# Scan loop of a hybrid RWKV encoder layer: fill matmuls between the first chunk's products, small products on four column groups, and later loads

## The chip, the cores and the metric

The kernel runs on one core of one Trainium2 chip. The metric is the time of one execution on the device, in microseconds. The time before is the median of three runs. In the profile PE is TensorE (PEld its weight loads), DVE is VectorE, ACT is ScalarE, POOL is GpSimd, and SP is SyncE, whose work here is the issuing of DMAs. Dies do not matter with one core.

## The reference, cut to what matters

Two request groups (1024 and 256 tokens of width 1024) pass one encoder layer with shared weights. A layer is a mixer (a gated short convolution and a bidirectional RWKV-7 recurrence, both fed from one input projection), a gated convolutional FFN, and a gated embedding. The change lies in the recurrence:

```
def step(S, inp):
    r_t, w_t, kk_t, b_t, k_t, v_t = inp
    sa = einsum('bhvk,bhk->bhv', S, kk_t)
    S = S * w_t - sa[..., None] * b_t + v_t[..., None] * k_t
    return S, einsum('bhvk,bhk->bhv', S, r_t)
...
for d, (z, z_shift, rev) in ((0, forward), (1, reverse)):
    outs.append(_wkv_scan(r, w, kk, kk * a, kd, v, rev))
y = outs[0] + outs[1]
```

There are 8 heads of size 64, two directions and 1280 tokens.

## The kernel before, in words

**Order.** The kernel is one long program. Nearly every instruction goes through a small wrapper class (`Pin`, its line is L204 in the profile) that keeps each engine's instructions in the order in which the Python code issues them. So every engine is a queue written by hand, and the order of calls in the code is the order of the work. SyncE issues nearly all DMAs, in order as well: a DMA that has to wait holds up the ones behind it.

**Scan.** The recurrence is computed in chunks of 64 tokens. A step n treats one group of 128 tokens (two chunks) in one direction: ten forward steps (n = 0 to 9), then ten backward ones (10 to 19). Within a chunk the recurrence needs the inverse of a triangular 64 by 64 matrix for each head. Its two diagonal 32 by 32 blocks are inverted on GpSimd (`b_inv`, 31 rounds of one product and one addition); the block beside them is put together with two small matrix products.

The functions of a step, and the tiles by which the profile shows them:

- `a_t(n)`: TensorE transposes of the keys K into two PSUM tiles (`g<-cst,K`), two copies to ZL on ScalarE.
- `a_gram(n, h)`, for each half h of the heads: Gram products of the keys with LS (`g<-LS,K`), six evictions on VectorE (AT, LS, ZL for each parity); after the second half the diagonal blocks go out to DRAM (dA). At h = 0 it also loads the start value W.
- `load_u(n)`: the blocks come back in another layout (U); `b_inv(n)` inverts them (W, tm).
- `b_out(n)`, `b_back(n)`: the inverses go to DRAM (dW) and come back (MT). `b_d(n)` transposes one quadrant of MT on VectorE (Dm).
- `b_x2(n)`: 16 products of 32 by 32 (`g<-Dm,AT`), called X^2 here, with the copy to X2 (in the profile X) on ScalarE. `b_m21(n)`: 16 more (`g<-MT,X`), M21, copied into MT.
- For each of the two chunks ci, in sequence because the second uses the state that the first leaves: `c_p1` (`p<-SV,LS`, copy R), `c_keep` (the old state, Sc), `c_sa` (`y<-SV,LS` and `p<-R,MT`, copied into SV), `c_z` (`p<-SV,ZL` and `y<-SV,ZL`; VectorE then forms the next state in Sc and SV, ScalarE copies Y).
- `load_k`, `load_l`, `load_v`: the loads of K (one buffer), LS (four buffers) and SV (two buffers) for later steps, on SyncE.

Inside step n the code works on three steps: the products of step n, the return of the inverse of step n+1 (`b_out`, `b_back`, `b_d`), and the Gram products and the inverse of step n+2. K and LS of step n+3 are loaded. PSUM has a ring of four tiles g for `a_t`, `a_gram`, `b_x2` and `b_m21`.

**Fill.** Between these pieces `gap(us, g)` runs matmuls of another stage, the rest of the input projection (`mm<-U,wh` and `mm<-U,wl`, in units of three matmuls, 0.65 us by the planner's table for 512 columns). The planner scales each gap by `share`, which is the work left, less a reserve TAIL, over the steps left and over 18.6, the sum of a step's gaps; a debt carries what a gap ran too much or too little. Fill brings its own weight splits and evictions on ScalarE and VectorE, its own loads on SyncE, and the queued side work that `run_side` issues. A gap with g set also issues a piece of the group norm of an earlier token group (steps 11 to 19), whose loads `gn_load` go through SyncE too.

**The lines that the change touches.** `a_gram` (L1100) and `a_t` (L1128): the place at which a ZL tile is made. `b_x2` (L1191) and `b_m21` (L1203). The prologue before the loop (L1340 to L1366): two `a_t`, `a_gram`, `load_u`, `b_inv`. The loop over n (L1374): `load_l(n + 3)` at its start, then `b_x2`, `c_p1(n, 0)`, `a_t(n + 2)`, `b_m21`, `c_keep`, `a_gram(n + 2, 0)`, `c_sa`, `a_gram(n + 2, 1)`, `c_z`, `load_u(n + 2)`, `b_inv(n + 2)`, a gap of 3.2, and the second chunk between gaps of 1.0, 1.5, 5.5 and 7.4. In the last two steps, which have no step n+2, gaps of 0.8, 1.0 and 1.0 stand in the places of `a_t` and the two `a_gram`.

Of the kernel before, what the change touches and what calls it, by code (L numbers as in the profile page):

```python
# [5 lines left out]
F32 = mybir.dt.float32  # L6
# [6 lines left out]
D = 1024  # L13
# [46 lines left out]
class B:  # L60
# [5 lines left out]
    def sb(self, pool, shape, dt=F32, tag=None, bufs=None):  # L66
        kw = {} if bufs is None else dict(bufs=bufs)
        return pool.tile(shape, dt, name=tag, tag=tag, **kw)
# [57 lines left out]
def build(tc, I, O, dbg=None, upto=99):  # L126
    b = B(tc, I, O)
    nc = tc.nc
    sb = b.sb
# [926 lines left out]
    ZL = {}  # L1056
# [10 lines left out]
    def load_k(n):  # L1067
        if n < N:
            d, g = steps[n]
            st[n] = dict(K=sb(wk, [128, 8, 128], F32, "K", 1))  # L1070
            (G if n == 0 else SP).dma_start(st[n]["K"].rearrange("p (h c) x -> p h (c x)", c=2), d_bk[d][:, g, :].rearrange("(h p) x -> p h x", p=128))

    def load_l(n):
        if n < N:
            d, g = steps[n]
            c, q = (d_cq[nm, d][:, g * 128:(g + 1) * 128].rearrange("(h p) x -> p h x", p=128) for nm in "cq")
            L = [LS[n % 4][:, i].rearrange("p (h c) t -> p h (c t)", c=2) for i in range(3)]
            e = G if n == 0 else SP
            for par in range(2):
                e.dma_start(L[par][halves[par]], c[halves[par]])  # L1080
            e.dma_start(L[2], q)
# [18 lines left out]
    def a_gram(n, h):  # L1100
        d, g = steps[n]
        S = st[n]
        if h == 0:
            S["AT"] = sb(wk, [128, 8, 64], F32, "AT", 3)
            S["dA"] = dr.tile([32, 32, 32], F32, name="dA", tag="dA", bufs=2)
            S["W"] = sb(wk, [128, 8, 32], F32, "W", 2)
            SP.dma_start(S["W"], I["consts"][:, C_WI:C_N].rearrange("p (c j) -> p c j", c=8))
        K, L, Zl, AT = S["K"], LS[n % 4], ZL[n % 3], S["AT"]
        bc = lambda c: cst[:, c:c + 64].unsqueeze(1).broadcast_to((128, 4, 64))
        MS, MQ = bc(C_MS[d]), bc(C_MQ[d])  # L1110
        pss = [sb(pg, [128, 4, 128], F32, "g") for par in range(2)]
        us = slice(4 * h, 4 * h + 4)
        for u in range(4):
            for par in range(2):
                rw = halves[par]
                PE.matmul(pss[par][:, u, :], K[rw, 4 * h + u, :], L[rw, par::2 - par, 4 * h + u, :], start=True, stop=True)
        cc, qc = slice(0, 64), slice(64, 128)
        for par in range(2):
            rw, ow, co, qo, ps = halves[par], halves[1 - par], par * 64, (1 - par) * 64, pss[par]
            V.tensor_tensor(AT[rw, us], ps[rw, :, cc], MS[rw], ALU.mult)  # L1120
            V.tensor_tensor(L[ow, par, us], ps[ow, :, cc], MS[ow], ALU.mult)
            V.tensor_tensor(Zl[:, par, us, qo:qo + 64], ps[:, :, qc], MQ, ALU.mult)
            if h == 1:
                for hh in range(2):
                    q = par * 2 + hh
                    SP.dma_start(S["dA"][q * 8:q * 8 + 8].rearrange("u s t -> s u t"), AT[q * 32:q * 32 + 32, :, hh * 32:hh * 32 + 32])

    def a_t(n):  # L1128
        if n < 3:
            ZL[n] = sb(wk, [128, 2, 8, 128], F32, f"ZL{n}")  # L1130
        K, Zl = st[n]["K"], ZL[n % 3]
        pss = [sb(pg, [128, 8, 64], F32, "g") for par in range(2)]
        for u in range(8):
            for par in range(2):
                PE.transpose(pss[par][:, u, :], K[halves[par], u, :], ident[halves[par], halves[par]])
        for par in range(2):
            A.copy(Zl[:, par, :, par * 64:par * 64 + 64], pss[par])

    def load_u(n):
        Ut = st[n]["U"] = sb(wk, [128, 32, 32], F32, "U", 2)  # L1140
        for r in range(4):
            SP.dma_start(Ut[r * 32:(r + 1) * 32], st[n]["dA"])


    def b_inv(n):
        d, g = steps[n]
        S = st[n]
        Ut = S["U"]
        W = S["W"]
        for i in (range(31) if d == 0 else range(31, 0, -1)):  # L1150
            cs = slice(0, i // 4 + 1) if d == 0 else slice(i // 4, 8)
            js = slice(i + 1, 32) if d == 0 else slice(0, i)
            nc_, nj = cs.stop - cs.start, js.stop - js.start
            tm = sb(wk, [128, 8, 32], F32, "tm", 1)
            G.tensor_tensor(tm[:, cs, js], W[:, cs, i:i + 1].broadcast_to((128, nc_, nj)),
                            Ut[:, i:i + 1, js].broadcast_to((128, nc_, nj)), ALU.mult)
            G.tensor_tensor(W[:, cs, js], W[:, cs, js], tm[:, cs, js], ALU.add)
# [33 lines left out]
    def b_x2(n):  # L1191
        d, g = steps[n]
        S = st[n]
        c1, c2, r1, r2 = quads(d)
        ps = sb(pg, [128, 4, 128], F32, "g")[:, 0:2, :].rearrange("p a (b j) -> p (a b) j", j=32)
        X2 = S["X2"] = sb(wk, [128, 8, 32], F32, "X2", 1)
        for u in range(8):
            for par in range(2):
                PE.matmul(ps[r2[par], u, :], S["AT"][r1[par], u, c2], S["D"][r1[par], u, :], start=True, stop=True)
        for par in range(2):  # L1200
            A.copy(X2[r2[par]], ps[r2[par]])

    def b_m21(n):  # L1203
        d, g = steps[n]
        S, Mt = st[n], MT[n % 2]
        c1, c2, r1, r2 = quads(d)
        ps = sb(pg, [128, 4, 128], F32, "g")[:, 0:2, :].rearrange("p a (b j) -> p (a b) j", j=32)
        for u in range(8):
            for par in range(2):
                PE.matmul(ps[r1[par], u, :], S["X2"][r2[par], u, :], Mt[r2[par], u, c2], start=True, stop=True)  # L1210
        for par in range(2):
            A.copy(Mt[r1[par], :, c2], ps[r1[par]])

    def chunks(n):
        return (0, 1) if steps[n][0] == 0 else (1, 0)
# [1 line left out]
    def c_p1(n, ci):  # L1217
        S, c = st[n], chunks(n)[ci]
        SV, L = S["SV"], LS[n % 4]
        ps1 = sb(pa, [128, 4, 64], F32, "p1")  # L1220
        for hp in range(4):
            for par in range(2):
                rw = halves[par]
                PE.matmul(ps1[rw, hp, :], L[:, par, 2 * hp + c, :], SV[:, c, par, hp, :], start=True, stop=True)
        R = S["R"] = sb(wk, [128, 4, 64], F32, "R", 1)
        A.copy(R, ps1)

    def c_keep(n, ci):
        S, c = st[n], chunks(n)[ci]
        Sc = S["Sc"] = sb(wk, [128, 4, 64], F32, "Sc", 1)  # L1230
        for par in range(2):
            A.copy(Sc[halves[par]], S["SV"][halves[par], c, par])
# [105 lines left out]
        SP.dma_start(d_ob[tk, :], v)  # L1338

    go(12.6)  # L1340
    a_t(0)
    for h in range(2):
        a_gram(0, h)
        go(1.2)
    load_u(0)
    b_inv(0)
    load_k(1)
    load_l(2)
    go(10.4)
    a_t(1)  # L1350
    for h in range(2):
        a_gram(1, h)
        go(1.2)
    load_u(1)
    load_k(2)
    b_inv(1)
    go(8.0)
# [9 lines left out]
    def gap(us, g=0):  # L1367
        k = max(1, round(us / 0.8))
        for _ in range(k):
            fill.run(us * share / k)  # L1370
            if g:
                next(gn, None)

    for n in range(N):  # L1374
        share = max(0.0, fill.left - TAIL) / (N - n) / 18.6
        nx, nx2 = n + 1 < N, n + 2 < N
        run_side()
        load_l(n + 3)
        if n == 4:
            gn_weights()  # L1380
        b_x2(n)
        c_p1(n, 0)
        if n >= 11:
            gn = group_norm(gl_g, gl_t)

        if nx2:
            a_t(n + 2)
        else:
            gap(0.8)
        b_m21(n)  # L1390
        c_keep(n, 0)
        if nx2:
            a_gram(n + 2, 0)
        else:
            gap(1.0)
        c_sa(n, 0)
        if nx2:
            a_gram(n + 2, 1)
        else:
            gap(1.0)  # L1400
        c_z(n, 0)
        if nx2:
            load_u(n + 2)
            b_inv(n + 2)
        if n >= 11:
            gn_load(gl_g, (2,))
        gap(3.2, 1)
        c_p1(n, 1)
        c_keep(n, 1)
        load_k(n + 3)  # L1410
        if nx:
            b_out(n + 1)
        gap(1.0, 1)
        c_sa(n, 1)
        if nx:
            b_back(n + 1)
        gap(1.5, 1)
        c_z(n, 1)
        fill.until(v_block + 1)
        if nx2:  # L1420
            load_v(n + 2)
        gap(5.5, 1)
        if nx:
            b_d(n + 1)
        gap(7.4, 1)
        for _ in gn:
            pass
        if n >= 10:
            gl_g = steps[n][1]
            gl_t = gn_load(gl_g, (0, 1, 3))  # L1430
# [644 lines left out]
```

## Time and profile before

| what | value |
|---|---|
| runs | 2170.63, 2177.81, 2175.63 us |
| median | 2175.63 us |
| profiled execution | 2179.25 us |
| its span, first to last instruction | 2177.5 us |
| mean granted TensorE clock | 0.993 |
| scan loop in the profiled execution | from 334 to about 884 us, 20 steps |

The rows of the profile read as follows. A timeline row has the start, the time from the first start to the last end, the engine, the operation, the tiles written and read, the shape and the count; in brackets the idle time before it and what ended it. A product with f32 operands of the small matrices appears as two passes, each with a weight load of its own, so 16 products are 32 rows. Matmuls overlap: the time that a group takes from the engine is the distance from its start to the next group's start. A row of the waits has the waiter, what it waited for, the total, the number of times and the longest. In a row of the stretches each engine's busy time is followed by its number of instructions, and the granted clock is a share of full speed.

### The profile page before, as it was taken

Reading aid. Unit: us, or ns where it says so; the run is one execution under the profiler, and the core shown is the slowest. Engines: PE = TensorE matmul, PEld = TensorE weight load, DVE = VectorE, ACT = ScalarE, POOL = GpSimd, SP = SyncE. Lnnn points to the kernel's source line nnn. Section 1 sums busy time; section 2 is a strip of 40 time slices with the busy share of each in tenths; the row PEclk is TensorE's granted clock in tenths of the full one; section 3 lists DMA queues with packets and bytes.
Section 4 is the critical chain, followed back from the end, with each engine's and each line's share of the span. In section 5 each row is a group of like instructions: output and inputs, shape, how many; then the busy total and the mean of one; then the engine's idle time right before and its main releaser. Section 6 shows DMA issues by size and latency. Waiting matters only on the chain.

```text
span 2177.5 us, 40081 instructions
## 1 busy us (share of the span) xinstructions
PE 2122.6 (97%) x15929; PEld 1842.6 (85%) x15929; DVE 1342.9 (62%) x2198; ACT 886.7 (41%) x1529; POOL 522.7 (24%) x1378
## 2 busy tenths in 40 slices
PE   6999999999999999999999999999999999999998
PEld 5877798888887787887889999999999888887886
DVE  5467823444445664565577677677777765556565
ACT  5556513333344444422455544444444511113444
POOL 4000046777776774000000000000000011125000
PEclk9999999999999999999999999999999999999999
DMA  4336675555566674635247422112223332233121
GB/s 154 111 102 179 178 209 126 129 139 133 124 180 179 177 195 139 234 124 168 96 131 205 141 77 76 64 64 77 70 76 121 145 109 87 87 114 114 44 85 54
DMA packets 345877, 273.16 MB, mean 125 GB/s; under 512 B 135549, under 2 KB 306907, under 8 KB 345691
## 3 DMA queue, kind: packets, MB, share of 16 engines
q1 hardware_dynamic: 332859, 245.96, 38.4%
q10 hardware_dynamic: 9632, 13.11, 1.7%
q0 software_dynamic: 3200, 11.54, 1.5%
q8 instruction: 125, 2.05, 0.4%
q14 instruction: 61, 0.50, 0.1%
HBM read 187.18 MB, written 83.36 MB: 124 GB/s over the span
## 4 chain that ended last, share of the span: by engine, by line
PE 60%; DVE 5%; DMA 3%; POOL 2%; issue 1%; ACT 1%; SPq 1%; ACTq 0%; DVEq 0%; POOLq 0%
PE mm L204 24%; PE X L204 13%; PE Y L204 10%; PE g L204 6%; PE m L204 3%; PE p L204 2%; POOL W L204 1%; POOL tm L204 1%; SPq L204 1%; DVE wl L204 1%; DVE h L204 1%; PE y L204 1%; PE tp L204 0%; DMA dW<-W 0%; DVE aj L204 0%
## 5 line engine op out<-in xcount | busy, mean ns | idle before, releaser
L204 PE MATMUL mm<-U,wh 128*128 128x512 f32 (+1 forms) x1872 | 519.4, 365 | 2.8 <-ACT U L204 2.3
L204 PEld LDWEIGHTS mm<-U,wh 128*128 128x128 f32 x1872 | 324.1, 189 | 68.7 <-issue 11.8
L204 PE MATMUL mm<-U,wl 128*128 128x512 f32 (+1 forms) x936 | 336.0, 359 | 1.0 <-POOL wl L204 1.0
L204 POOL TENSOR_TENSOR tm<-W,U 128x60 f32<-128x60 f32 (+24 forms) x620 | 200.4, 323 | 111.4 <-DMA U<-dA 63.6
L204 POOL TENSOR_TENSOR W<-W,tm 128x60 f32<-128x60 f32 (+24 forms) x620 | 214.4, 346 | 48.6
L204 PEld LDWEIGHTS mm<-U,wl 128*128 128x128 f32 x936 | 176.8, 189 | 29.4 <-POOL wl L204 1.6
L204 DVE TENSOR_TENSOR f<-f,mm 128x512 f32<-128x512 f32 x200 | 136.4, 686 | 101.5 <-PE mm L204 100.4
L204 POOL TENSOR_TENSOR MG<-raw,MG 128x1024 fp32r<-128x1024 f32 x5 | 12.1, 2413 | 654.2 <-ACT MG L204 654.2
L204 PE MATMUL X<-B,wh 128*128 128x384 f32 (+1 forms) x936 | 158.5, 315 | 2.9 <-DVE MGb L204 2.9
L204 DVE SCALAR_TENSOR_TENSOR h<-MGb,fcol,h 128x255 f32<-128x255 f32 (+1 forms) x176 | 152.6, 880 | 14.1 <-ACT h L204 12.3
L204 ACT CAST wh<-raw 128x512 fp32r<-128x512 f32 (+1 forms) x141 | 113.8, 808 | 116.4 <-PE Y L204 41.6
L204 PE MATMUL mm<-MG,act 128*128 128x512 f32 x600 | 158.6, 391 | 0.7 <-DVE f L204 0.6
L204 PEld LDWEIGHTS X<-B,wh 128*128 128x128 f32 x936 | 144.3, 189 | 3.4 <-DVE MGb L204 3.4
L204 PE MATMUL X<-B,wl 128*128 128x384 f32 (+1 forms) x804 | 137.2, 315 | 3.1 <-DVE MGb L204 2.9
L204 PEld LDWEIGHTS mm<-MG,act 128*128 128x128 f32 x600 | 112.9, 189 | 24.8 <-DVE f L204 1.4
L204 PEld LDWEIGHTS X<-B,wl 128*128 128x128 f32 x804 | 123.7, 190 | 3.7 <-DVE MGb L204 3.1
L204 PE MATMUL mm<-wh,MG 128*128 128x512 f32 x400 | 126.3, 394 | 0.0
L204 PE MATMUL g<-WG,MG 128*128 128x512 f32 x480 | 112.8, 391 | 0.0
L204 PEld LDWEIGHTS g<-WG,MG 128*128 128x128 f32 x480 | 89.4, 188 | 18.3
L204 DVE TENSOR_TENSOR AT<-g,cst 64x256 f32<-64x256 f32 x80 | 33.6, 420 | 106.9 <-PE g L204 105.9
L204 DVE TENSOR_TENSOR wl<-raw,wh 128x1024 fp32r<-128x1024 f32 (+1 forms) x68 | 75.2, 1106 | 34.8 <-ACT wh L204 34.4
L204 PEld LDWEIGHTS mm<-wh,MG 128*128 128x128 f32 x400 | 74.8, 187 | 18.5
(503 smaller groups left out, 4178.7 us busy)
## 6 DMA issues: line engine op xcount, KB each, us to landing
raw<-in_w_up SPq DMA_DIRECT2D x53, 512.0 KB
raw<-in_w_in SPq DMA_DIRECT2D x39, 512.0 KB
d_act<-h SPq DMA_DIRECT2D x22, 640.0 KB
MGb<-d_act SPq DMA_DIRECT2D x20, 640.0 KB
raw<-in_w_down SPq DMA_DIRECT2D x22, 512.0 KB
d_bk<-o SPq DMA_DIRECT2D x32, 320.0 KB
U<-dA SPq DMA_DIRECT2D x80, 128.0 KB
K<-d_bk SPq DMA_DIRECT2D x19, 512.0 KB
```

Of the source, the lines that this page charges most:

```text
L204: return lambda *a, **k: tc.keep_in_program_order(f(*a, **k))
```

## The change

1. X^2 and M21. So far the sixteen products write two column groups (32 partitions of PSUM each) and 256 columns. Now heads-and-chunks u = 0 to 3 go to the column groups used so far and u = 4 to 7 to the other two, in the order u, u + 4, so that products of both row groups and all four column groups follow one another; the result has 128 columns. The copy is split: ScalarE takes the first four, VectorE the other four.
2. Order of a step. `a_t(n + 2)` goes from between `c_p1(n, 0)` and `b_m21(n)` to behind `c_keep(n, 1)`. Gaps of 1.3, 0.6 and 1.0 come in before `b_m21`, before `c_sa(n, 0)` and before `c_z(n, 0)`; the gap behind `b_inv` shrinks from 3.2 to 2.4, those of 5.5 and 7.4 to 4.9 and 5.9. The sum stays 18.6. The special gaps of the last two steps are gone.
3. `load_l(n + 3)`, the three loads of LS, goes from the start of the step to behind `b_inv(n + 2)`.
4. Prologue: the first two `a_t` go behind the `a_gram` and `load_u` of their step (the first also behind `b_inv`).

```
     def b_x2(n):
-        ps = sb(pg, [128, 4, 128], F32, "g")[:, 0:2, :].rearrange("p a (b j) -> p (a b) j", j=32)
+        ps = sb(pg, [128, 4, 128], F32, "g")[:, 0, :].rearrange("p (b j) -> p b j", j=32)
-        for u in range(8):
-            for par in range(2):
-                PE.matmul(ps[r2[par], u, :], S["AT"][r1[par], u, c2], S["D"][r1[par], u, :], start=True, stop=True)
+        for u in range(4):
+            for v, r in ((u, r2), (u + 4, r1)):
+                for par in range(2):
+                    PE.matmul(ps[r[par], u, :], S["AT"][r1[par], v, c2], S["D"][r1[par], v, :], start=True, stop=True)
         for par in range(2):
-            A.copy(X2[r2[par]], ps[r2[par]])
+            A.copy(X2[r2[par], 0:4], ps[r2[par]])
+            V.tensor_copy(X2[r2[par], 4:8], ps[r1[par]])
...
     for n in range(N):
         run_side()
-        load_l(n + 3)
...
         b_x2(n)
         c_p1(n, 0)
+        gap(1.3)
...
-        if nx2:
-            a_t(n + 2)
-        else:
-            gap(0.8)
         b_m21(n)
         c_keep(n, 0)
         if nx2:
             a_gram(n + 2, 0)
-        else:
-            gap(1.0)
+        gap(0.6)
         c_sa(n, 0)
         if nx2:
             a_gram(n + 2, 1)
-        else:
-            gap(1.0)
+        gap(1.0)
         c_z(n, 0)
         if nx2:
             load_u(n + 2)
             b_inv(n + 2)
+        load_l(n + 3)
...
-        gap(3.2, 1)
+        gap(2.4, 1)
         c_p1(n, 1)
         c_keep(n, 1)
+        if nx2:
+            a_t(n + 2)
         load_k(n + 3)
...
-        gap(5.5, 1)
+        gap(4.9, 1)
         if nx:
             b_d(n + 1)
-        gap(7.4, 1)
+        gap(5.9, 1)
```

`b_m21` is changed as `b_x2` is, with the roles of r1 and r2 exchanged and the copies going into MT.

More of the change, by code (lines that the diff above doesn't have):

```diff
@@ L1103, in a_gram @@
         if h == 0:
+            if n < 3:
+                ZL[n] = sb(wk, [128, 2, 8, 128], F32, f"ZL{n}")
             S["AT"] = sb(wk, [128, 8, 64], F32, "AT", 3)
@@ L1128, in a_t @@
     def a_t(n):
-        if n < 3:
-            ZL[n] = sb(wk, [128, 2, 8, 128], F32, f"ZL{n}")
         K, Zl = st[n]["K"], ZL[n % 3]
@@ L1206, in b_m21 @@
         c1, c2, r1, r2 = quads(d)
[L1207 to L1210, printed above, removed]
+        ps = sb(pg, [128, 4, 128], F32, "g")[:, 0, :].rearrange("p (b j) -> p b j", j=32)
+        for u in range(4):
+            for v, r in ((u, r1), (u + 4, r2)):
+                for par in range(2):
+                    PE.matmul(ps[r[par], u, :], S["X2"][r2[par], v, :], Mt[r2[par], v, c2], start=True, stop=True)
         for par in range(2):
-            A.copy(Mt[r1[par], :, c2], ps[r1[par]])
+            A.copy(Mt[r1[par], 0:4, c2], ps[r1[par]])
+            V.tensor_copy(Mt[r1[par], 4:8, c2], ps[r2[par]])
     def chunks(n):
@@ L1340, in build @@
     go(12.6)
-    a_t(0)
     for h in range(2):
@@ L1346, in build @@
     b_inv(0)
+    a_t(0)
     load_k(1)
@@ L1349, in build @@
     go(10.4)
-    a_t(1)
     for h in range(2):
@@ L1354, in build @@
     load_u(1)
+    a_t(1)
     load_k(2)
```

## Prediction

> **What bounds the kernel now.** I read the page first, then the busy time by stretches with one stretch for each scan step, then TensorE's own timeline through step 9, and last the waits that end inside the loop. All edits are in the scan loop, so the page only has to say which engine to watch.
>
> ```profile
> span 2177.5 us, 40081 instructions
> ...
> PE 2122.6 (97%) x15929; PEld 1842.6 (85%) x15929; DVE 1342.9 (62%) x2198; ACT 886.7 (41%) x1529; POOL 522.7 (24%) x1378
> ```
>
> The columns of the stretches: limits, length, busy time of each engine, granted clock, DMA share, GB/s. Step 9 starts at 577.89, steps 12, 13 and 14 at the next three starts; the last row lies inside step 13.
>
> ```profile
> core 0: us, PE busy (x) PEld busy (x) DVE busy (x) ACT busy (x) POOL busy (x), PEclk, DMA share, GB/s
> 577.89:604.50 26.61, 26.48 (x350) 22.11 (x350) 15.01 (x28) 8.03 (x19) 21.75 (x63) 1.00 0.37 88
> 658.47:687.59 29.12, 26.98 (x357) 22.20 (x356) 15.79 (x35) 13.04 (x27) 20.03 (x62) 1.00 0.64 174
> 687.59:718.26 30.67, 29.63 (x359) 25.25 (x359) 19.51 (x41) 13.52 (x27) 22.32 (x62) 0.89 0.67 178
> 718.26:748.90 30.64, 28.70 (x366) 23.93 (x366) 18.81 (x40) 13.40 (x27) 21.36 (x60) 0.94 0.65 177
> ...
> 689.00:695.50 6.50, 6.50 (x130) 5.91 (x133) 3.06 (x5) 3.71 (x9) 5.48 (x14) 0.50 0.73 213
> ```
>
> In step 9 TensorE is busy 26.48 of 26.61 us, so an ordinary step is TensorE's instruction list from end to end: a gain must shorten that list. GpSimd, which does the 32-row inverses, is busy 21.75 us of the step and runs close behind. Steps 12 to 14 are 2.5, 4.1 and 4.0 us longer than step 9, and one stretch runs at clock 0.50: there are the real stalls, 10.6 us in all.
>
> TensorE's list in step 9 (start, time to the last end, form, count):
>
> ```profile
> 575.69 0.63 PE L204 MATMUL mm<-U,wh 128*128 128x512 f32 x2
> ...
> 576.39 0.63 PE L204 MATMUL mm<-U,wh 128*128 128x512 f32 x2
> ...
> 577.89 0.69 PE L204 MATMUL g<-Dm,AT 32*32 32x32 f32 x32
> 578.51 0.69 PE L204 MATMUL p<-SV,LS 128*64 128x64 f32 x16
> 579.13 0.71 PE L204 MATMUL g<-cst,K 64*128 64x64 f32 x16
> 579.77 0.69 PE L204 MATMUL g<-MT,X 32*32 32x32 f32 x32
> 580.39 1.27 PE L204 MATMUL g<-LS,K 64*128 64x128 f32 x16
> 581.60 0.27 PE L204 MATMUL y<-SV,LS 64*64 64x64 f32 x2
> ...
> 582.24 1.16 PE L204 MATMUL g<-LS,K 64*128 64x128 f32 x16
> 583.33 0.69 PE L204 MATMUL p<-SV,ZL 128*64 128x64 f32 x16
> ...
> 584.41 0.50 PE L204 MATMUL mm<-U,wh 128*128 128x256 f32 x2
> ...
> 587.58 1.04 PE L204 MATMUL p<-SV,LS 128*64 128x64 f32 x16
> 588.55 0.73 PE L204 MATMUL mm<-U,wh 128*128 128x512 f32 x2
> ...
> 590.13 0.27 PE L204 MATMUL y<-SV,LS 64*64 64x64 f32 x2
> ...
> 590.75 0.73 PE L204 MATMUL mm<-U,wh 128*128 128x512 f32 x2
> ```
>
> In order: X^2 (b_x2), c_p1, the transposes of a_t, M21, the Gram products of half 0, c_sa, Gram half 1, c_z, fill; then the second chunk's c_p1 and c_sa between fill. Start to start these take 0.62, 0.62, 0.64, 0.62, 1.21, 0.64, 1.09, 1.08 us. Each counted matmul is one pass; 32 passes are 16 instructions of the program.
>
> **The change, part by part.** Negative is a gain.
>
> (A) *X^2 and M21 on four column groups.* Same passes, four array tiles in flight instead of two. Turn time from the rows: c_z runs its 32 passes of 64 columns on two tiles, 16 turns, in 1.08 us; c_p1 has 8 such turns in 0.62. The difference gives 0.0575 us a turn and 0.16 us fixed. X^2 has 16 turns of 32 columns in 0.62, so 0.029 us a turn. Does a turn hold four tiles for the price of two? The second chunk's c_sa answers: it runs 32 passes of 64 columns on a 2 by 2 set of tiles, from 590.13 to 590.75, 0.62 us, exactly c_p1's 0.62 for half as many passes. So four tiles fit, each row group feeding two column groups, as the new loops have it. X^2 then takes 8 x 0.029 + 0.16 = 0.39, a gain of 0.23; twice a step, 20 steps: **-9.2**. The other end is 0, if passes cannot start faster than X^2's present one per 0.016 us. The row of c_sa is one per 0.014 at twice the columns, so I take the whole gain. The Trainium skill, "TensorE: Matmul & The Clock Gate", section "Wait — 56ns, not 53.3ns?", has a floor of about 25 ns between matmul starts; by it nothing would be gained here and the sum below would be +0.7 instead of -8.5; but 32 passes in 0.62 us are under that floor already, so the trace does not agree.
>
> (B) *Fill between the first chunk's products.* a_t is taken out from between c_p1 and M21, and fill goes in at three places (before M21, before c_sa, before c_z). The total is unchanged, 18.6 in units of a step, so only the added entries cost. An entry is priced in step 18, where fill already stands between c_p1 and M21:
>
> ```profile
> 831.70 0.72 PE L204 MATMUL mm<-U,wh 128*128 128x512 f32 x2
> ...
> 832.59 0.69 PE L204 MATMUL g<-MT,X 32*32 32x32 f32 x32
> ```
>
> Three matmuls take 0.89 there and 0.70 in the stream (575.69 to 576.39): 0.19 an entry, 3 x 0.19 x 18 steps = **+10.3**. Steps 18 and 19 already had the three. If the 0.6 gap is often empty it is +6.8. a_t costs TensorE the same 0.64 in its new place.
>
> (C) *The second chunk's c_p1.* At 587.58 it takes 0.97 to its successor, not 0.62. What it waits for:
>
> ```profile
> 587.94 0.54 PEld L204 LDWEIGHTS p<-SV,LS 128*64 128x64 f32 x14 [0.20 <-DVE SV L204]
> ...
> 581.59 0.42 DVE L204 TENSOR_TENSOR AT<-g,cst 64x256 f32<-64x256 f32 x1 [3.61 <-PE g L204]
> ...
> 586.48 0.41 DVE L204 TENSOR_TENSOR Sc<-p,Sc 128x256 f32<-128x256 f32 x1
> 586.92 0.97 DVE L204 TENSOR_TENSOR SV<-Sc,pend 64x256 f32<-64x256 f32 x2
> ```
>
> VectorE starts the first Gram eviction at 581.59 and works without a break through twelve of them, Sc and SV until 587.89: 6.3 us after Gram half 0, while TensorE needs 587.58 - 581.60 = 6.0 to arrive. In the new order TensorE needs, from the same point, 0.79 (0.6 of fill and an entry) + 0.64 + 1.09 + 1.19 + 1.08 + 2.59 = 7.4. The wait of 0.35 is covered by 1.1 us, unless fill's own VectorE work, now issued between the evictions, eats it. 0.35 in some 15 steps is 5.3; bounds 0 and -5.3; I take 70%, **-3.7**.
>
> (D) *First-half waits.* Gram half 0 takes 1.21, half 1 1.09 for the same sixteen passes: its second PSUM tile is one that a_t filled just before and ScalarE still empties. With a_t in the second chunk the four-deep ring comes round to tiles long free: 0.12 x 18 = **-2.2**. In the backward steps c_sa takes 0.79 (below) against 0.64, as it waits for M21's copies; fill now stands before it and VectorE takes half of them: 0.15 x 8 = **-1.2**.
>
> ```profile
> 608.21 0.27 PE L204 MATMUL y<-SV,LS 64*64 64x64 f32 x2
> ...
> 609.00 1.16 PE L204 MATMUL g<-LS,K 64*128 64x128 f32 x16
> ```
>
> (E) *The queue of SyncE.* Three loads of LS move behind the twelve of W, dA and U (SyncE, all DMAs in order) and ahead of K and dW. a_t issues no DMA, but load_k now waits for its transposes, 0.64 us after c_p1; behind that wait stand K and dW, and for dW wait MT, Dm, and X^2 of the next step.
>
> ```profile
> 594.44 2.56 SPq L204 DMA_DIRECT2D dW<-W  x4
> 598.80 1.80 SPq L204 DMA_DIRECT2D MT<-dW  x4
> ...
> 664.58 1.28 SPq L204 DMA_DIRECT2D LS<-d_c  x2
> 665.90 0.60 SPq L204 DMA_DIRECT2D LS<-d_q  x1
> ...
> 676.34 2.55 SPq L204 DMA_DIRECT2D dW<-W  x4
> ...
> 684.93 1.82 SPq L204 DMA_DIRECT2D MT<-dW  x4
> ```
>
> ```profile
> PE g L204 <- DVE Dm L204: 4.5, 5, 2.1
> ...
> ACT R L204 <- DMA LS<-d_c: 3.8, 1, 3.8
> ```
>
> LS costs the queue 1.9 us. In step 12 it stands before dA when the queue is already late, so dA and U come up to 1.9 us earlier now; but dW keeps its place behind LS, so the end of the chain moves little. In step 12 dW took 684.93 - 678.89 = 6.0 us to land against 1.8 in step 9, X^2 came late and the clock fell to 0.50. In step 14 ScalarE's R stood 3.8 us behind a landing of LS that now comes at another time. These are collisions in the DMA queues: some will go, others come. Their sum is the 10.6 us of the three steps and a part of the 2.4 us by which the waits for Dm exceed their longest (4.5 less 2.1); I count 1.4 of these, so 12.0. Bounds: -12 and, by the slower rival, +16. I take a third back, **-4.0**.
>
> (F) *New copies on VectorE.* Four a step, each at most the 0.42 of an eviction twice as wide; before Gram half 0 VectorE is idle (3.61 us ahead of 581.59), and 1.3 us of fill and c_p1 lie between X^2 and M21. Where group norm is queued ahead (steps 11 to 19) M21 can wait: between 0 and 0.97 (two queued operations such as SV's) x 8 = 7.8; I take **+1.5**, as 0.62 + 1.49 us of work cover most.
>
> (G) *Prologue.* The two first a_t move behind their Grams; no fill is added, bound one a_t either way, 0.64. I take 0.
>
> Sum: -9.2 + 10.3 - 3.7 - 2.2 - 1.2 - 4.0 + 1.5 = -8.5. The profiled execution took 2179.25 us (span 2177.5), so 2170.75 there; it lies 3.6 above the median of the three runs, 2175.63, and against that median the forecast is **2167.1 us**.
>
> **The rivals.**
>
> *Packing gains nothing.* X^2's passes already start 0.016 us apart (half of a turn's 0.029 us), and if starts are limited by issue there, four tiles change nothing. Against it stands c_sa's 0.014 with columns twice as long. Sum -8.5 + 9.2 = +0.7: 2176.3. The floor named in (A) is of this kind.
>
> *The late stalls all go.* For it: the queue is 1.9 us freer before dA just where it is late. Then (E) is -12.0 and (C) -5.3, sum -18.1: 2157.5.
>
> *Slower: LS in front of dW.* In every step dW is now issued directly behind LS and K, 1.9 us later in the queue, and may land as slowly as in step 12, 4.2 us later. This row is the slack at step 10, which starts at 604.50:
>
> ```profile
> 602.06 0.44 DVE L204 STREAM_TRANSPOSE Dm<-MT 32x256 f32<-32x256 f32 x1 [0.65 <-DMA MT<-dW]
> ```
>
> 2.0 us. It decides once 1.9 plus the added landing time exceeds 2.0; at the full 6.1, X^2 is 4.1 late. Half of that in eight backward steps is +16, and (E)'s -4 falls away: sum -8.5 + 4 + 16 = +11.5: 2187.1. Against it: GpSimd is busy 21.75 of a step's 26.61 us, so the end of an inverse, rather than the queue, mostly lets dW go.
>
> That the change does not do what it says is excluded: all its instructions are issued in a fixed order.
>
> **How the numbers follow.** A measurement of this kernel tells about 0.3%, 6.5 us, from no change. Chances: my sum, give or take 5 us, 0.60 (two thirds of it more than 6.5 below); packing gains nothing 0.12; late stalls all go 0.16; slower 0.12. Faster by over 0.3%: 0.40 + 0.16 = 0.56; slower 0.12; the rest, 0.32, is within. The range runs from the second rival, 2157, to just past the first with a small share of the third, 2179; left out are most of the slower rival and what lies below all-stalls-gone, under 2 in 10.
>
> **What would show it.** X^2 and M21 at 0.39 start to start instead of 0.62 (A); fill between M21 and c_sa with three matmuls in 0.89 (B); the second chunk's c_p1 at 0.62 (C); Gram half 0 at 1.09 (D); ordinary steps about 0.3 us shorter than now; in the waits, TensorE behind Dm at or under 4.5 us. Wrong would be X^2 still at 0.62, or Dm waits in many steps with SyncE's dW later than 16 us after the step's start.

## The result and the profile after

The changed kernel is slower: 2200.51 us (median of five, 2196.18 to 2203.96) against 2172.76 us (median of five) before, a ratio of 1.0127 with a 95% interval of 1.0112 to 1.0141. That is 27.7 us more, where 8.5 less was forecast. The profiled execution took 2200.83 us; the one before lies 6.5 above its median, so the two profiles are only 21.6 us apart. The span after, then the stretches of five steps (9, 7, 11, 12, 13, each from one X^2 to the next) and 2 us out of step 7; the columns are those of the table of stretches in the prediction:

```profile
span 2199.0 us, 40124 instructions
```

```profile
580.57:607.66 27.09, 26.45 (x350) 21.55 (x349) 16.05 (x32) 7.63 (x19) 22.16 (x63) 1.00 0.44 113
524.30:554.08 29.78, 27.96 (x341) 22.21 (x340) 14.25 (x28) 8.31 (x20) 22.17 (x66) 0.94 0.47 126
634.96:666.79 31.83, 27.06 (x357) 21.35 (x357) 15.81 (x38) 13.23 (x27) 20.72 (x64) 0.99 0.58 163
666.79:697.69 30.90, 29.38 (x356) 23.15 (x356) 18.93 (x42) 12.51 (x26) 19.90 (x60) 0.90 0.60 167
697.69:731.06 33.37, 31.01 (x360) 24.82 (x360) 20.79 (x45) 13.11 (x27) 20.39 (x58) 0.85 0.59 160
529.60:531.60 2.00, 2.00 (x19) 1.78 (x17) 0.58 (x2) 1.31 (x4) 1.61 (x6) 0.50 0.96 294
```

Step 9, an ordinary step, takes 27.09 us (26.61 before), where 0.3 less was expected. Steps 11 to 13 take 31.83, 30.90 and 33.37 (26.90, 29.12 and 30.67 before). Seven steps, 11 to 17, carry most of the loss: from X^2 of step 11 to X^2 of step 18 it is 854.22 - 634.96 = 219.3 us, against 829.68 - 631.57 = 198.1 before, 21.2 us more. Among the steps before these, step 7 alone loses 3.2. The same seven steps as one stretch, after and then before:

```profile
634.96:854.22 219.26, 201.45 (x2488) 159.72 (x2489) 132.14 (x294) 91.09 (x187) 147.60 (x426) 0.93 0.60 167
631.57:829.68 198.11, 192.63 (x2490) 159.90 (x2489) 121.51 (x263) 94.45 (x187) 146.41 (x420) 0.97 0.68 184
```

Of the 21.2 us, 12.3 are standing (17.8 against 5.5). The other 8.8 are busy time: TensorE takes that much longer for the same number of matmuls, at a mean granted clock of 0.93 instead of 0.97. So a part of the cost is slower matmuls, as in step 7 below, behind a stand.

What TensorE waited for, in all:

```profile
PE g L204 <- DVE Dm L204: 14.5, 12, 3.5
...
PE g L204 <- ACT X L204: 5.6, 6, 1.8
```

Dm was late for 4.5 us in the whole run before, and now for 14.5. The copies of X are a wait that the page before did not have.

**Where the copies hurt.** Step 7, all engines but SyncE, in order of time:

```profile
523.15 3.21 DVE L204 SCALAR_TENSOR_TENSOR cvy<-cvp,pcol,cvy 128x1282 f32<-128x1282 f32 x2
...
524.30 0.45 PE L204 MATMUL g<-Dm,AT 32*32 32x32 f32 x32
...
524.83 0.26 ACT L204 COPY X<-g 32x128 f32<-32x128 f32 x1 [5.79 <-PE g L204]
...
526.28 1.34 DVE L204 TENSOR_TENSOR wl<-raw,wh 128x1024 fp32r<-128x1024 f32 x1
...
527.55 0.68 DVE L204 TENSOR_TENSOR cvy<-mm,cvy 128x512 f32<-128x512 f32 x1
...
528.26 0.28 DVE L204 COPY X<-g 32x128 f32<-32x128 f32 x1
...
528.57 0.26 ACT L204 COPY X<-g 32x128 f32<-32x128 f32 x1 [3.48 <-DVE X L204]
...
528.86 0.29 DVE L204 COPY X<-g 32x128 f32<-32x128 f32 x1 [0.32 <-ACT X L204]
...
528.88 0.76 PE L204 MATMUL g<-MT,X 32*32 32x32 f32 x30 [1.75 <-ACT X L204]
...
529.57 2.08 PE L204 MATMUL g<-LS,K 64*128 64x128 f32 x16
```

X^2 is through at 524.7. ScalarE copies its first quarter at once. VectorE has a convolution, a weight split and an eviction of fill queued ahead, and takes its first quarter at 528.26, 3.5 us later. ScalarE's second quarter then stands 3.48 us behind VectorE's first: the four copies go one after another, ScalarE, VectorE, ScalarE, VectorE. TensorE stands still for 1.75 us, the clock falls to 0.50 (last row of the stretches), and the Gram half behind it takes 2.08 instead of 1.16.

**Where the loads hurt.** Step 11. GpSimd's inverse, then SyncE's issues, then what SyncE waited for between 652 and 661, then TensorE's first product of step 12:

```profile
647.08 0.29 POOL L204 TENSOR_TENSOR W<-W,tm 128x8 f32<-128x8 f32 x1
653.56 0.36 POOL L204 TENSOR_TENSOR tm<-W,U 128x31 f32<-128x31 f32 x1 [6.20 <-DMA U<-dA]
```

```profile
649.33 1.71 SPq L204 DMA_DIRECT2D U<-dA  x4
651.08 1.24 SPq L204 DMA_DIRECT2D LS<-d_c  x2
652.36 0.61 SPq L204 DMA_DIRECT2D LS<-d_q  x1
653.01 0.51 SPq L204 DMA_DIRECT2D cvy<-d_v  x1
653.62 0.41 SPq L204 DMA_DIRECT2D K<-d_bk  x1
659.87 2.56 SPq L204 DMA_DIRECT2D dW<-W  x4
663.92 1.87 SPq L204 DMA_DIRECT2D MT<-dW  x4
```

```profile
SPq L204 <- DMA d_thr<-gth: 5.8, 1, 5.8
```

```profile
666.79 0.31 PE L204 MATMUL g<-Dm,AT 32*32 32x32 f32 x2 [3.50 <-DVE Dm L204]
```

The inverse that dW waits for ends at 647.37, but dW goes out at 659.87, 12.5 us later. U, LS, cvy and K stand ahead of it, and between K and dW SyncE waits 5.8 us until another transfer has landed (the profile names an output of fill, issued by ScalarE; in the trace that output and the first transfer of dW report to the same semaphore, so the wait is probably for its reuse, which no run tests). In step 11 before, it went out 3.1 us behind the inverse's end at 642.86, straight behind K:

```profile
645.35 0.53 SPq L204 DMA_DIRECT2D K<-d_bk  x1
645.97 2.71 SPq L204 DMA_DIRECT2D dW<-W  x4
```

Over the nine inverses of steps 11 to 19, dW went out 1.30 us behind the end of the inverse on average before, and 6.40 now; over the nine of steps 2 to 10 it was 0.31 and 2.09. The landing did not get slower: from the last issue of dW to the first of MT it took 2.6 us on average before and 2.2 after, in steps 11 to 19.

### The profile page after: what moved, and what is told of

It reads as the page before. It is cut to its first block, busy times and chain, and to the rows that moved or that the text cites. A ratio compares the mean times of both kernels' runs of the same rounds, so it can differ in the third digit from the quotient of the medians.

```text
span 2199.0 us, 40124 instructions
## 1 busy us (share of the span) xinstructions
PE 2128.9 (97%) x15929; PEld 1832.7 (83%) x15929; DVE 1366.9 (62%) x2278; ACT 878.7 (40%) x1529; POOL 521.6 (24%) x1378
## 4 chain that ended last, share of the span: by engine, by line
PE 62%; DVE 6%; DMA 4%; POOL 2%; ACT 2%; issue 2%; SPq 1%; ACTq 0%; POOLq 0%; DVEq 0%
PE mm L204 25%; PE X L204 13%; PE Y L204 10%; PE g L204 7%; PE m L204 3%; PE p L204 2%; SPq L204 1%; POOL W L204 1%; POOL tm L204 1%; PE y L204 1%; DMA dW<-W 1%; DMA MT<-dW 1%; DVE wl L204 1%; DMA U<-dA 1%; DMA dA<-AT 1%
## 5 line engine op out<-in xcount | busy, mean ns | idle before, releaser
L204 PE MATMUL mm<-U,wh 128*128 128x512 f32 (+1 forms) x1872 | 529.3, 370 | 2.8 <-ACT U L204 2.3
L204 PEld LDWEIGHTS mm<-U,wh 128*128 128x128 f32 x1872 | 323.1, 190 | 71.3 <-issue 12.5
L204 PE MATMUL Y<-B,wh 128*128 128x384 f32 x420 | 85.1, 335 | 0.0
```

Source lines behind the costliest of these rows:

```text
L204: return lambda *a, **k: tc.keep_in_program_order(f(*a, **k))
```

## The experiments

Ratios are to the kernel before, with their 95% intervals. The first theory has two causes: the divided copies, and the loads of LS ahead of dW. The rival is the rest of the change: packing, the moved transposes, and fill cut into more pieces. "After" is the changed kernel, "before" the old one.

**Undoing each in the changed kernel.** Three versions of after: all eight copies on ScalarE (a_act), the loads of LS back at the start of the step (a_ls), and both (a_act_ls); and before with the packing alone (b_pack_act, all copies on ScalarE).

```
a_act        -            V.tensor_copy(X2[r2[par], 4:8], ps[r1[par]])
             +            A.copy(X2[r2[par], 4:8], ps[r1[par]])       (and the same for MT)
a_ls         -        load_l(n + 3)      (behind b_inv(n + 2))
             +        load_l(n + 3)      (behind run_side())
```

> The changed kernel with all eight copies of X^2 and M21 back on ScalarE. Theory 'copies' (the halves on VectorE wait behind its queue, and because the four copies read one PSUM bank they run ScalarE, VectorE, ScalarE, VectorE in turn; M21 is late and everything behind it): most of the 27.7 us over the kernel before goes, about 2178 to 2186, and M21's waits for X go. Theory 'loads' (LS in front of K and dW makes Dm late): 5 us at most go, about 2196, and the waits of TensorE for Dm stay near 15 us.

> The changed kernel with the three loads of LS back at the start of the step. Theory 'loads': about 2175 to 2183, TensorE's wait for Dm falls from 14.5 us to under 6. Theory 'copies': under 6 us go, about 2195, waits for Dm and X stay. A third theory, 'fill' (fill between the first chunk's products brings weight loads and VectorE work ahead of dA), expects little from this run and from the one with the copies on ScalarE.

> Both: copies on ScalarE and LS at the start of the step. If 'copies' and 'loads' are the whole cause, the forecast's structural sum shows: 2163 to 2172, under the kernel before. Theory 'fill': stays above 2180.

> The kernel before with X^2 and M21 on four column groups and nothing else, all copies on ScalarE. X^2 at 0.38 us start to start. If packing is worth its full price, 2162 to 2166 (0.24 us twice a step, 9.6 us). If the longer copies (four of 0.26 us for two of 0.37) delay M21, which has only c_p1 and a_t before it, 2168 to 2174.

Measured: a_act 1.0067 (1.0046 to 1.0088), a_ls 1.0047 (1.0026 to 1.0069), a_act_ls 1.0006 (0.9993 to 1.0019), b_pack_act 0.9996 (0.9985 to 1.0007). In medians, taking away the copies gives back 2200.5 - 2187.1 = 13.4 us, the loads 2200.5 - 2181.9 = 18.6, and both 26.0 of the 27.7, less than the sum: the two losses overlap by about 6. With the other one already gone, the copies cost 7.4 and the loads 12.6. So both are shown as causes, and the rest of the change is worth nothing that can be measured. Neither theory for a_act held as put, with 13.4 us between "most" and 5; a_ls fits the theory of the loads, and a_act_ls missed its range of 2163 to 2172 with 2174.5. In the traces M21 shows the copies' cost directly: from its start to that of the next stage it takes 17.8 us over the loop in a_ls, and 8.1 in a_act_ls. Packing gains nothing as a whole either, though X^2 and M21 together fell from 29.3 us over the loop to 19.9 in b_pack_act: Gram half 0 went from 22.5 to 29.5 us (start to start 1.6 in nearly every step, where it was 1.2), which by the order of the work is a wait for PSUM tiles that ScalarE, with eight copies a step, still empties (not tested by itself). Its time lies in the range forecast for longer copies, but what waits is Gram and not M21. Here it is in step 10, 1.68 us, where step 9 before had 1.27:

```profile
603.80 0.46 PE L204 MATMUL g<-MT,X 32*32 32x32 f32 x32
604.19 1.68 PE L204 MATMUL g<-LS,K 64*128 64x128 f32 x16
```

**Doing each alone in the kernel before**, and two versions that ask how: b_ls (only the loads moved), b_pack_dve (only the packing, copies divided), a_ls_2bank (a_ls, with the two halves of X^2 and M21 in two PSUM tiles, so that the engines need not take turns), a_act_lsm (a_act, with the loads behind those of MT).

```
a_ls_2bank   -        ps = sb(pg, [128, 4, 128], F32, "g")[:, 0, :]...
             +        pss = [sb(pg, [128, 4, 128], F32, "g")[:, 0, :]... for _ in range(2)]
a_act_lsm    -        load_l(n + 3)      (behind b_inv(n + 2))
                          b_back(n + 1)
             +        load_l(n + 3)
```

> The kernel before, with the loads of the next step's LS issued where the changed kernel issues them (behind dA and U, ahead of K and dW) and nothing else changed. Theory 'the loads stand in front of dW': each step's dW goes out about 2 us later behind the end of GpSimd's inverse, as it did in the changed kernel (2.1 us in the forward steps, 6.4 in the backward ones, against 0.3 and 1.3 before), TensorE waits for Dm longer than the 4.5 us in sum of before, and the run takes 10 to 18 us more than the kernel before, that is a ratio of 1.005 to 1.008. Rival 'the loads hurt only where the raw weight loads of the added fill blocks are in the same queue': a ratio of 0.998 to 1.002, waits for Dm at most 6 us in sum.

> The kernel before, with X^2 and M21 on four column groups and with the copies divided between ScalarE and VectorE as the changed kernel has them; fill, a_t and loads stay as before. The same packing with all copies on ScalarE took 0.9996 of the time before. Theory 'divided copies of one PSUM tile go one after another and stand in VectorE's queue behind other work': M21 waits for X in the steps with group norm, 3 us and more in the sum of 'PE behind X', and the run takes 5 to 13 us more than with the copies on ScalarE: a ratio of 1.002 to 1.006. Rival 'the divided copies only hurt where fill feeds VectorE between X^2 and M21': a ratio of 0.996 to 1.001, since VectorE then also takes load off ScalarE, behind which Gram waited.

> The changed kernel with all eight copies on ScalarE and the loads of LS issued behind the loads of MT, so that neither dA and U nor dW stand behind them; a transfer of LS then has about half a step less time. The same with the loads at the start of the step took 1.0006. Theory 'what counts is what stands in front of dA, U and dW in the queue of SyncE': 3 to 7 us below that, a ratio of 0.997 to 0.999, waits for Dm below 9.5 us in sum. Rival 'the chain over GpSimd's inverse sets the length of the backward steps': within 0.2% of 1.0006. If LS lands too late, ScalarE's R and the products of the next step wait for it and the ratio is above 1.003.

> The changed kernel with the loads of LS back at the start of the step, copies divided between the two engines as in the changed kernel, but with the two halves of X^2 and of M21 in two PSUM tiles, so that a copy of VectorE and one of ScalarE need not wait for each other. With one tile it took 1.0047, with all copies on ScalarE 1.0006. Theory 'the four copies of one PSUM tile run as a chain': 1.000 to 1.002, ScalarE's waits behind VectorE's copies of X gone. Rival 'the copies on VectorE stand behind group norm and its fill work in VectorE's own queue': 1.003 to 1.006, waits of TensorE for X and for the copies remain, now behind VectorE.

Measured: b_ls 1.0070 (1.0046 to 1.0094), b_pack_dve 1.0025 (1.0011 to 1.0038), a_act_lsm 1.0034 (1.0022 to 1.0045), a_ls_2bank 1.0042 (1.0027 to 1.0057). Each cause does its harm alone. TensorE's wait for Dm and SyncE's queue in step 12 of b_ls:

```profile
PE g L204 <- DVE Dm L204: 11.1, 10, 3.6
```

```profile
678.58 1.25 SPq L204 DMA_DIRECT2D LS<-d_c  x2
679.88 0.60 SPq L204 DMA_DIRECT2D LS<-d_q  x1
680.53 0.50 SPq L204 DMA_DIRECT2D cvy<-d_v  x1
681.14 0.41 SPq L204 DMA_DIRECT2D K<-d_bk  x1
687.54 2.60 SPq L204 DMA_DIRECT2D dW<-W  x4
```

The same 6 us between K and dW as in after, with no fill entry added. So the added entries are not needed for it.

Two tiles for the halves do not help: 1.0042 against 1.0047. ScalarE no longer waits for VectorE's copies (26.0 us in a_ls, none here), but TensorE waits for X as long as in a_ls, 6.2 us, now for VectorE. VectorE in step 12 of a_ls_2bank, then TensorE's waits in all:

```profile
660.42 0.69 DVE L204 TENSOR_TENSOR cvp<-cvp,gnb 128x512 f32<-128x512 f32 x1
661.03 0.80 DVE L204 TENSOR_TENSOR cvy<-cvy,bon 128x512 f32<-128x512 f32 x1
661.86 0.72 DVE L204 TENSOR_TENSOR cvp<-cvp,cvy 128x512 f32<-128x512 f32 x1
662.62 0.69 DVE L204 TENSOR_TENSOR cvy<-cvp,cvy 128x512 f32<-128x512 f32 x1
663.22 1.35 DVE L204 TENSOR_TENSOR wl<-raw,wh 128x1024 fp32r<-128x1024 f32 x1
```

```profile
PE g L204 <- DVE X L204: 6.2, 7, 1.7
```

X^2 ends at 660.9; group norm's last four operations and a weight split of fill, until 664.57, are ahead of the copy. M21, with its wait, takes 17.7 us over the loop, against 17.8 in a_ls. So what holds M21 is VectorE's queue; the turns that the engines take on one tile have no share that shows, though the intervals leave room for some us.

The expectation for a_act_lsm failed in its first two theories. LS now landed too late: TensorE waited for LS four times, 3.0 us, and for Dm 10.2 us. Here the loads want to be early, not only out of dW's way.

**Is it the chain over the inverse?** One version for the gain that does not show: a_1fill, which is a_act_ls with one added fill entry a step in place of three. And a test of the theory that GpSimd's inverse, through dW, MT and Dm, sets the backward steps: before, a_1fill and after, each with the last 4 of the 31 rounds of every inverse left out (b_short, a_1fill_short, after_short).

```
a_1fill      -        gap(0.6)        (before c_sa(n, 0))
             -        gap(1.0)        (before c_z(n, 0))
             -        gap(2.4, 1)
             +        gap(4.0, 1)
..._short    -        for i in (range(31) if d == 0 else range(31, 0, -1)):
             +        for i in (range(27) if d == 0 else range(31, 4, -1)):
```

> The changed kernel with the copies of X^2 and M21 on ScalarE, the loads of LS back at the start of the step, and one added fill entry in place of three: fill stays between c_p1 and M21, the fill on both sides of c_sa goes to the stretch behind c_z. With three entries it took 1.0006. The trace of that run shows 52 more entries of fill than before and 18.6 us more time in fill for it, about 0.27 us an entry and 4 to 5 us of waits at their ends; everything else took 18.9 us less. Theory 'the gains are real and the entries eat them': 35 entries fewer give back 9 us or more, a ratio of 0.995 to 0.997, 2158 to 2163 us. Rival 'the chain over GpSimd's inverse sets the backward steps, so that what TensorE saves there turns into waiting for Dm': only the forward steps gain, 4 us at most, a ratio of 0.998 to 1.001, with more waits for Dm than the 9.5 us of the run with three entries.

> The kernel before, with the last 4 of the 31 row steps of each inverse on GpSimd left out (part of the computation is left out). An inverse of 25.5 us becomes some 3 to 4 us shorter. Theory 'the chain over the inverse holds up the backward steps in the kernel before': the three steps of 29 to 31 us shrink towards 27 and the waits for Dm, 4.5 us, go: 4 to 12 us less, a ratio of 0.994 to 0.998. Rival 'those steps are long for other reasons': within 0.2% of 1.

> The one-entry version with the same 4 row steps of each inverse left out. Theory 'the chain hides in the backward steps what TensorE saves': with the shorter inverse the saving shows in all steps, 10 to 16 us below the kernel before with the shorter inverse. Rival 'the savings are lost elsewhere on TensorE': less than 5 us below it.

> The changed kernel with the same 4 row steps of each inverse left out. Theory 'late loads cost their 18.6 us through the chain dW, MT, Dm': with 3 to 4 us of slack in that chain most of it goes, while the 13.4 us of the copies, which do not go over the inverse, stay: 0 to 12 us above the kernel before with the shorter inverse, waits for Dm under 6 us. Rival 'the loads cost by contention or on another path': still 20 us or more above it.

Measured: a_1fill 0.9990 (0.9978 to 1.0002), b_short 0.9992 (0.9980 to 1.0003), a_1fill_short 0.9977 (0.9966 to 0.9989), after_short 1.0118 (1.0105 to 1.0132). This theory fell, on all three. The inverses became about 3 us shorter (25.5 to 22.2 for those of steps 2 to 10 in b_short), and after_short is as slow as after, with the same wait for Dm. (In b_short's trace the three long steps did shrink, to 27.55, 27.89 and 29.90 us, but the time did not fall clear of noise.) TensorE's wait for Dm in after_short:

```profile
PE g L204 <- DVE Dm L204: 14.4, 11, 3.9
```

In after_short dW only goes out longer behind the end of the inverse, 9.04 us on average for those of steps 11 to 19, against 6.40. So what holds dW is SyncE's queue, and not the inverse. a_1fill gave 3.5 us in place of the 9 expected of the entries theory. By the traces fill did take 7.2 us less than in a_act_ls (362.7 against 369.9), but the two c_sa of a step took 6.8 us more, 4.0 of them the first c_sa of steps 18 and 19, which now have no fill ahead of them: there the fill had covered waits. Against the kernel before, the steps up to 10 became 4.7 us shorter in sum and the later ones longer, while the waits for Dm fell to 5.9 us, which the rival had not expected.

**Place, bytes, or both?** Three ways of taking something away ahead of dW: a_act_lsq (a_act, the loads of LS issued by ScalarE's queue), a_act_k (a_act, K behind dW) and b_k (before, K behind dW). And a_1fill_k, a_1fill with K behind dW.

```
a_act_lsq    -        load_l(n + 3)
             +        load_l(n + 3, A)
..._k        -        load_k(n + 3)
                      if nx:
                          b_out(n + 1)
             +        load_k(n + 3)
```

> The changed kernel with all copies on ScalarE, in which the three loads of LS are issued at the same place of the step but from ScalarE's queue. With them in SyncE's queue it took 1.0067, with them at the start of the step 1.0006. Theory 'place in the queue': K and dW go out 1.9 us earlier, waits for Dm fall from 19.3 us to under 12 us, a ratio of 1.000 to 1.003 (ScalarE's own 1.9 us of issuing a step may cost 1 to 3 us of it). Rival 'bytes and landings': 512 KB of LS still land between U and dW, dW still waits; a ratio of 1.004 to 1.008.

> The changed kernel with all copies on ScalarE, and the load of K issued behind the four of dW in place of ahead of them; the loads of LS stay late. Theory 'bytes and landings ahead of dW': half of the bytes that were ahead of dW are gone, dW goes out up to 6 us earlier in the backward steps, a ratio of 1.001 to 1.004. Rival 'place behind LS': dW gains only the 0.6 us of K's issue, a ratio of 1.005 to 1.007.

> The kernel before with the load of K issued behind the four of dW. In its trace dW lands slowly in two steps (MT 5 to 6 us behind dW's last issue instead of 1.4), with K's 512 KB ahead. Theory 'bytes ahead of dW': the long steps 12 to 14 of 29 to 31 us lose 1 to 3 us each, a ratio of 0.997 to 0.999. Rival 'K only comes later': 0.999 to 1.002, with waits of Gram for K.

> The one-entry version (copies on ScalarE, loads of LS at the start of the step, one added entry), with the load of K behind dW. Without that it took 0.9990. Theory 'bytes ahead of dW keep the gain from showing in the backward steps': their steps of 28 to 30.5 us fall to 27 to 28, a ratio of 0.994 to 0.997. Rival: 0.998 to 1.000.

Measured: a_act_lsq 1.0013 (1.0001 to 1.0025), a_act_k 1.0035 (1.0023 to 1.0047), against 1.0067 of a_act; b_k 0.9971 (0.9957 to 0.9985); a_1fill_k 0.9974 (0.9962 to 0.9986), above its theory's range by a little. Taking LS out of SyncE's queue gives back nearly all of its cost, with waits for Dm of 6.4 us in place of 19.3. It is not a clean test of place against bytes, since ScalarE reaches its loads earlier: in steps 11 to 16 LS goes out 9 to 14 us into the step, and not 15 to 19. Taking K's 512 KB away gives back half. Over the inverses of steps 11 to 19 dW went out 5.9 us behind the inverse's end in a_act, 2.6 in a_act_k and 0.4 in a_act_lsq, while it landed about as fast (2.6, 2.0 and 2.2 us); so the loss lies ahead of dW's issue. In the kernel before, where LS does not stand directly ahead of dW, K behind dW gains too. What SyncE waited for in the scan loop, before and in b_k:

```profile
SPq L204 <- DMA dW<-W: 41.3, 27, 5.4
```

```profile
SPq L204 <- DMA dW<-W: 20.3, 26, 1.9
```

SyncE waits for dW before it can issue MT. With K's 512 KB issued ahead, the four 32 KB transfers of dW took 41.3 us of waiting over the loop, at worst 5.4; with K behind them 20.3, at worst 1.9. Moving K changes its place and the bytes ahead of dW at once, so how the gain divides between them stays open. b_k and a_1fill_k are faster than the kernel before, by 0.29% and 0.26%.

## Why the prediction was wrong

**(A) Right in size.** X^2 and M21 take 0.39 each in step 9 of after, as predicted:

```profile
580.57 0.45 PE L204 MATMUL g<-Dm,AT 32*32 32x32 f32 x32
580.96 0.69 PE L204 MATMUL p<-SV,LS 128*64 128x64 f32 x16
581.57 0.51 PE L204 MATMUL mm<-U,wh 128*128 128x256 f32 x2
...
583.19 0.45 PE L204 MATMUL g<-MT,X 32*32 32x32 f32 x32
583.58 1.16 PE L204 MATMUL g<-LS,K 64*128 64x128 f32 x16
584.67 0.50 PE L204 MATMUL mm<-U,wh 128*128 128x256 f32 x2
```

That is 32 passes in 0.39 us, one each 12 ns; the rival that packing gains nothing by the rate of starts is refuted. So is, for these passes, the floor of about 25 ns between matmul starts in the Trainium skill, "TensorE: Matmul & The Clock Gate", section "Wait — 56ns, not 53.3ns?". The evidence for (A) was thinner than it was put: four tiles in a turn of 0.029 us need a start each 7 ns, c_sa had shown one each 14, and its 32 passes take the same 0.62 us as those of X^2. That the whole gain came, and not a part, was in part luck. In a_act_ls, without the two causes of harm, X^2 and M21 take 8.0 us less over the loop, of 9.2 predicted.

**(B) The price of an entry was right, the waits at its end were left out: +10.3 became about +18.6.** The fence shows Gram half 0 at 1.09 (583.58 to 584.67) and an entry of three matmuls: 0.55 from 584.67 to 585.22, of matmuls with 256 columns, three of which take 0.35 in the stream. Over the loop the time from fill's first matmul to the next stage was 351.3 us in 85 entries before and 369.9 in 137 entries in a_act_ls. With each matmul priced as in the stream (0.23 us with 512 columns, 0.12 with 256), an entry costs 0.20 us by the median in both kernels, against 0.19 forecast; 52 entries, rather than 54, make 10.4. The rest, about 8, lies in a few entries: 15 of a_act_ls cost more than 0.5 us beside their matmuls, where two did before, because TensorE waits at their ends for Dm or SV, or runs them at a clock of 0.50 after such a wait. The sum put these waits at nothing. TensorE's busy time in fill's matmuls over the loop, before, in a_act_ls, and in a_1fill, grows with the number of entries (85, 137 and 99):

```profile
334.20:871.40 537.20, 353.83 (x1697) 275.43 (x1696) 14.46 (x24) 24.81 (x47) 0.99 0.58 152
```

```profile
333.00:870.00 537.00, 368.27 (x1687) 274.04 (x1686) 14.29 (x24) 24.35 (x46) 0.99 0.58 152
```

```profile
332.90:868.50 535.60, 358.66 (x1688) 275.46 (x1687) 14.32 (x24) 24.34 (x46) 0.99 0.58 152
```

**(C), (D) Right as sums.** The second chunk's c_p1 lost 3.3 us over the loop in a_act_ls (3.7 predicted), Gram half 0 lost 2.5 (2.2) and the first c_sa 1.0 (1.2). In step 9 itself (C) failed: c_p1 still waits for the state, 0.58 us (in after). Taken together (A) to (D) were to give 6.0 us and gave nothing that can be measured, and the missing part is the waits in (B).

**(E) Failed: -4.0 became +12.6 to +18.6 (without and with the divided copies).** Two sentences of the prediction were wrong. "dW keeps its place behind LS, so the end of the chain moves little" took the loads at the start of a step to be as much ahead of dW as those just in front of it. In step 12 before, they were issued by 666.50 and had until 676.34 to land; in the new place they have no such time. And "the end of an inverse, rather than the queue, mostly lets dW go", the argument against the slower rival, was read off GpSimd's busy share. It held for the inverses of steps 2 to 10, with dW 0.31 us behind. For those of steps 11 to 19 the profile before had 1.30 already, with the queue of SyncE late; after_short shows that the inverse is not what sets dW there. The slower rival named the right place, LS in front of dW, and its 16 us are close to what the loads cost. It split them otherwise: it had dW 1.9 us later in the queue and landing up to 4.2 us more slowly, and the runs show it 5.1 us later in the queue, and landing as fast. So its size is in part luck. Its chance of 0.12 was too small, and it did not have the copies.

**(F) Failed: +1.5, bounds 0 to 7.8, became +7.4 to +13.4 (without and with the late loads).** The bound counted two operations ahead of a copy, by the duration of SV's. In step 7 there are 5.2 us of them (3.21, 1.34 and 0.68), 3.5 of them still to do when X^2 is through, and M21 has to wait for the copies that stand behind them. In nine steps of after, two of them without group norm, M21 takes over 0.5 us longer than its 0.38. "0.62 + 1.49 us of work cover most" set the cover against a short queue; the fill put in as cover brings VectorE work itself. In step 7 the clock fell to 0.50 after the wait, which made it dearer than its own length.

**(G)** Nothing in the runs speaks for a cost of the prologue: X^2 of step 0 starts at 334.10, and at 334.22 before.

Of the signs named, (A) and (D) came. The sign of being wrong came as well, TensorE waiting for Dm 12 times and dW going out more than 16 us into the step; but that limit does not tell the kernels apart, since dW was at 16.55 us in step 9 before.

## What to carry to other kernels

Before a copy goes to the engine that is less busy on average, list what is queued ahead of it in each of the steps concerned: a queue of 3.5 us in step 7, and waits in nine of twenty steps, cost more here than the balanced share saved. In a queue of DMAs that issues in order, look at what stands directly ahead of the small transfer that the next step waits for: large loads that are needed late go behind it, and no load that can go early is moved in front. A saving on the busiest engine is worth only what remains once the pieces into which the work is cut, and the waits at their ends, are paid for.

## What was not expected of the hardware

Four 32 KB transfers behind one of 512 KB cost SyncE 41.3 us of waiting over twenty steps, and 20.3 with that one moved behind them. After a stand of 1.75 us TensorE's granted clock was 0.50 in the next stretch of 2 us, so that a Gram half of 1.16 took 2.08.
